# A hybrid attention layer on one core: lower parts of the memory weights on VectorE, sample queries stored once, own places for short pairs, first mix rows and output weights loaded two steps ahead

## The chip, the core and the metric

The kernel runs on one core of a Trainium2 chip. A core has TensorE (PE, matrix products; its weight loads are shown as PEld), VectorE (DVE), ScalarE (ACT) and GpSimd (POOL), and SyncE (SP), from whose queue this kernel issues all its DMA transfers. The metric is the device time in microseconds (us) of one execution; a time is the median of several runs.

## The reference, cut to what matters

One layer of a streaming encoder, for a prompt of 1024 frames and a sample (decode) group of 64 frames that share the weights. Everything is in 32-bit floats, model width 1024.

```
h  = rms_norm(x, g1);  one projection h @ w_in -> q, k, v of 8 heads A and 8 heads B, and forget logits
oa = band attention (chunk + 8 previous chunks, relative bias)       # prompt; sample: 512 cached keys + 64
ob = forgetting attention (bias = cumulated log sigmoid, causal)     # prompt; sample: 1024 cached keys + 64
x  = x + concat(oa, ob) @ w_o
mk, mv = split(rms_norm(mem_prompt, g_mem) @ w_mkv);  mk = rms_norm(mk)     # 256 memory rows; prompt only
x  = x + attend(rms_norm(rms_norm(x, g2) @ w_mq), mk, mv) @ w_mo
x  = x + (silu(causal_conv(gate)) * value) @ w_down,   gate, value = rms_norm(x, g3) @ w_up
```

Outputs: both groups' y, the new keys, values and forget logs, the memory keys and values, the convolution's state.

## The kernel before, in words

**Products in parts.** Most products are computed from two rounded parts of each operand, `hi` (rounded, by ACT) and `lo` (the remainder: raw minus `hi`, by DVE or POOL), in three products `hi*hi`, `hi*lo`, `lo*hi`.

**Stages.** (1) Projection and prompt attention, pair by pair: eight pairs `p` of two heads (0 to 3 are A, 4 to 7 are B). The sample's 64 frames are projected behind the prompt's; `proj_sample` (L353) normalises their queries and keys in a tile `qk` of four heads (two of q, two of k), in which every 64 numbers stand twice (`a` in `p h a d`), and its `store` (L376) writes them to a buffer `sqk` in HBM, and the values to `sv`. (2) From about 572 us on, the memory projection (L637), woven with the last prompt heads and then with the eight sample pairs. (3) The output product with `w_o` (L951), from 686 us on, then memory queries, memory attention, `w_mo`, the feed-forward layer.

**Memory projection.** `w_mkv` is cut into eight blocks `n` of 256 columns; for each block there are two row tiles `t`, and each (n, t) has four pieces of six matmuls. A list `line` holds the 64 pieces, and one entry more for the last key tile. The four quarters `y` of a block's weights are split ahead by `split_wm(n, y)` (L623): ACT writes `hi` (tile `mwhi`, L629), and `lo` (tile `mwlo`, L630) goes to DVE for odd `y` and to POOL for even `y`. Block 0 is split beside the last projection, block n+1 in the pieces of (n, t = 1).

**Sample pairs.** `Sample.load` (L756) brings queries and keys (`sqd`), new values (`svn`), cached keys (`kraw`) and cached values (`vraw`), all on SP. `prep` (L783) has POOL copy two heads at a time out of the doubled layout into `pair` (L789), PE transpose them (L790) into a bank `tq`, ACT and DVE scale the result (L795, L796); for pairs of kind B POOL also adds to the bias rows (L799, L802). `score` (L805) makes the logits and the exponential (L813 to L826), `turn` and `sum` transpose the probabilities and multiply by the values (L837 to L851, scaled at L857), `out` writes the mixed rows to `smix` (L861, L863). The pairs run in the order `SAMPLES = (4, 7, 5, 6, 0, 1, 3, 2)`: the first four from pool `mp`, the last four, which have the short cache of 512 keys, from pool `mq`. A loop over `x` from 0 to 8 takes one pair in each step; it loads pair x + 3 and gives each step `PER[x]` pieces of the memory line. With these numbers the memory line ends with step 6.

**The opening of the output product.** In step 7, `open_left` (L979) closes the left pools and opens on their place the weight stream (`Stream`, L915, raw tiles `raw`, three places, parts made at L932 and L933), the parts `a` of the mixed rows and the raw places `mraw` (`STAGE` = 10). The prompt's mixed rows lie in an HBM buffer `mixd`, eight tiles of 128 rows; they are taken in three chunks of columns (`CHUNKS`), so 24 loads `n`, chunk by chunk. Ten are loaded at once, and `split_mix(n)` (L998; ACT L1001, DVE L1002) loads n + 10 behind itself. The first product, chunk 0 of output tile 0, needs the eight split rows of that chunk and two weight tiles of `w_o`.

**What sets the order.** Each engine runs its queue in order. The program's order is a starting point: the queues are laid out when the program is built, and an instruction can stand before one that the code has earlier. `weave` and `place` spread secondary work over the pieces of a product. `tc.issue_after` keeps the loads in its block behind a given transfer.

## Time and profile before

| | |
|---|---|
| Median of 3 runs | 1759.43 us (1755.65 to 1760.1) |
| The profiled execution | 1761.79 us, of which the span is 1760.0 us |
| Mean granted clock of TensorE | 0.995 |
| Busy share PE, PEld | 97%, 94% |
| Busy share DVE, ACT, POOL | 67%, 52%, 36% |
| DMA | 196.70 MB, mean 112 GB/s |
| Memory projection (L637) | 572.0 to 679.4 us |
| Sample pairs' scores (L813) | 611.5 to 681.9 us |
| Output product (L951, first matmul) | 686.1 us |

How to read the rows. A timeline row gives start, duration, engine, line, operation, out<-in by the program's names, the number of merged instructions, and in brackets the idle time before it with what ended it. A waits row gives the total in us, the times, the longest. A stretch row gives start and end, length, busy time of PE, PEld, DVE, ACT and POOL with their instructions, the granted clock of TensorE, the mean busy share of the 16 DMA engines, and GB/s. A transfer row gives the count, KB each, and the median us from issue to landing. "SPq" is SP's queue.

### The profile page before, as it was taken

What the parts mean: (1) busy time and instruction counts of PE and PEld (TensorE: products, weight loads), DVE (VectorE), ACT (ScalarE), POOL (GpSimd) and SP (SyncE); (2) the same over time, 40 slices, a digit from 0 to 9 for tenths busy, and PEclk for the clock granted to TensorE, in tenths of its full rate; (3) what the DMA queues carried; (4) which work ended last, traced back from release to release, by engine and by line L of the source; (5) the groups of instructions that cost most, each with busy time, mean ns of one, the idle gap of its engine ahead of it and who ended that gap; (6) DMA issues with size and microseconds to landing.
All of it is one profiled execution on the core that took longest, in us unless ns stands there. A gap on an engine that the chain in (4) does not pass through costs nothing.

```text
span 1760.0 us, 33766 instructions
## 1 busy us (share of the span) xinstructions
PE 1700.5 (97%) x12376; PEld 1652.9 (94%) x12376; DVE 1180.9 (67%) x2591; ACT 920.2 (52%) x2030; POOL 629.4 (36%) x933
## 2 busy tenths in 40 slices
PE   7898999999999999999999999999999999999999
PEld 6788999999998888999999999999999999999999
DVE  5768667677677745333444389777777777659996
ACT  6756667677677656434555455433333334434442
POOL 3557667779778531553433512000000000000000
PEclk9999999999999999999999999999999999999999
DMA  7322222222233676531112662222222222793332
GB/s 253 93 64 59 66 73 72 62 75 62 61 105 95 200 218 207 183 116 43 49 54 69 176 214 72 92 80 86 82 74 74 75 74 74 255 337 120 113 105 88
DMA packets 135670, 196.70 MB, mean 112 GB/s; under 512 B 21240, under 2 KB 77688, under 8 KB 135504
## 3 DMA queue, kind: packets, MB, share of 16 engines
q1 hardware_dynamic: 135504, 194.55, 35.2%
q8 instruction: 97, 1.59, 0.4%
q14 instruction: 69, 0.57, 0.1%
HBM read 152.20 MB, written 45.44 MB: 112 GB/s over the span
## 4 chain that ended last, share of the span: by engine, by line
PE 46%; DVE 4%; issue 2%; ACT 1%; DMA 1%; POOL 1%; SPq 0%; DVEq 0%; ACTq 0%; POOLq 0%
PE W L1481 25%; PE W L1805 10%; PE pj L951 7%; PE S L1224 1%; PE tq L1260 1%; PE O L1260 1%; POOL lo L933 1%; DVE f L1346 1%; PE PT L1247 0%; DVE lo L1346 0%; ACT hi L1345 0%; DMA f<-x2d 0%; PE O L1224 0%; DMA x2d<-qhi 0%; DMA raw<-in_w_down_dram 0%
## 5 line engine op out<-in xcount | busy, mean ns | idle before, releaser
L310 PE MATMUL pj<-whi,xhi 128*128 128x384 f32 (+1 forms) x512 | 194.1, 379 | 2.3 <-DVE flog L325 1.6
L310 PE MATMUL pj<-wlo,xhi 128*128 128x384 f32 (+1 forms) x512 | 175.7, 343 | 4.5 <-POOL wlo L131 4.3
L310 PE MATMUL pj<-whi,xlo 128*128 128x384 f32 (+1 forms) x512 | 174.8, 342 | 0.7 <-DVE xlo L139 0.7
L1587 POOL COPY s<-gp 128x2 f32<-128x2 f32 x22 | 15.8, 720 | 335.9 <-DVE gp L1586 335.9
L1481 PE MATMUL W<-h,hi 128*128 128x272 f32 x704 | 134.4, 288 | 1.4 <-ACT qlo L1617 1.4
L515 ACT ACTIVATE s<-s,mx 128x640 f32<-128x640 f32 (+7 forms) x128 | 94.4, 738 | 75.4 <-DVE mx L513 74.7
L1805 PE MATMUL W<-f,hi 128*128 128x272 f32 x672 | 127.3, 287 | 0.0
L552 DVE TENSOR_TENSOR ptl<-PT,pth 128x512 fp32r<-128x512 f32 (+2 forms) x192 | 99.5, 522 | 35.5 <-ACT pth L551 33.6
L1481 PEld LDWEIGHTS W<-h,hi 128*128 128x128 f32 x704 | 110.8, 188 | 1.7 <-ACT qlo L1617 1.6
L1805 PEld LDWEIGHTS W<-f,hi 128*128 128x128 f32 x672 | 105.3, 188 | 0.2
L551 ACT CAST pth<-PT 128x512 fp32r<-128x512 f32 (+2 forms) x192 | 84.9, 449 | 38.9 <-PE PT L550 37.2
L310 PEld LDWEIGHTS pj<-wlo,xhi 128*128 128x128 f32 x512 | 98.5, 192 | 6.4 <-POOL wlo L131 6.0
L310 PEld LDWEIGHTS pj<-whi,xhi 128*128 128x128 f32 x512 | 98.3, 192 | 4.1 <-DVE flog L325 1.9
L1481 PE MATMUL W<-h,lo 128*128 128x272 f32 x352 | 101.8, 289 | 0.0
L310 PEld LDWEIGHTS pj<-whi,xlo 128*128 128x128 f32 x512 | 97.3, 190 | 1.8 <-DVE xlo L139 1.6
L1805 PE MATMUL W<-f,lo 128*128 128x272 f32 x336 | 96.8, 288 | 0.2 <-DVE lo L1346 0.2
L1345 ACT CAST hi<-raw 128x512 fp32r<-128x512 f32 x68 | 42.2, 621 | 102.2 <-PE W L1481 59.0
L550 PE MATMUL PT<-ident,s 128*128 128x128 f32 x528 | 89.6, 275 | 5.3 <-DVE ptl L552 5.3
L510 PE MATMUL S<-kh,q 128*128 128x256 f32 (+1 forms) x304 | 76.5, 277 | 16.6 <-DVE mx L513 16.5
L951 PE MATMUL pj<-a,hi 128*128 128x384 f32 (+1 forms) x352 | 86.9, 332 | 3.4 <-ACT hi L932 2.6
L518 POOL TENSOR_SCALAR s<-s,ssum 128x640 f32<-128x640 f32 (+6 forms) x96 | 70.8, 738 | 41.1 <-DVE ssum L516 30.0
L550 PEld LDWEIGHTS PT<-ident,s 128*128 128x128 f32 x528 | 65.4, 140 | 14.9 <-DVE ptl L552 9.1
(542 smaller groups left out, 5933.0 us busy)
## 6 DMA issues: line engine op xcount, KB each, us to landing
raw<-in_w_down_dram SPq DMA_DIRECT2D x45, 256.0 KB, 3.0
wraw<-in_w_dram SPq DMA_DIRECT2D x56, 192.0 KB, 2.5
raw<-in_w_up_dram SPq DMA_DIRECT2D x41, 256.0 KB, 2.8
h<-ad SPq DMA_DIRECT2D x32, 272.0 KB, 5.3
mwraw<-in_w_mkv_dram SPq DMA_DIRECT2D x16, 512.0 KB, 4.6
raw<-in_w_mo_dram SPq DMA_DIRECT2D x32, 256.0 KB, 3.3
kvraw<-in_w_down_dram SPq DMA_DIRECT2D x32, 256.0 KB, 3.5
ad<-t SPq DMA_DIRECT2D x22, 272.0 KB, 2.1
```

Source lines behind the costliest of these rows:

```text
L310: pe.matmul(pj[:, :nw], x_part(a, k, t * P, P), wt[k][b][:, :nw], start=n == 0, stop=n == 3 * KT - 1)
L510: pe.matmul(sp[:, a:a + (k1 - k0) * P], q, kk[:, h, src], start=m == 0, stop=m == 1)
L515: act.activation(s[:, :n], s[:, :n], ACT.Exp, bias=mx, scale=-1.0, accum_out=sm)
L518: pool.tensor_scalar(s[:, :n], s[:, :n], sm, 1.0, op0=ALU.mult, op1=ALU.mult)
L550: pe.transpose(pt[:, b - ch[0]], self.s[j][:, (b - w0) * P:(b - w0 + 1) * P], ident)
L551: act.copy(hi[:, f:f + n, j], pt[:, f:f + n])
L552: dve.tensor_tensor(lo[:, f:f + n, j], pt[:, f:f + n], f32(hi[:, f:f + n, j]), op=ALU.subtract)
L951: pe.matmul(out()[:, :cn], w[a][:, k % 4], x[b][k][:, c0:c0 + cn], start=k == 0 and (a, b) == SPLIT[0], stop=k == KT - 1 and (a, b) == SPL ...
L1260: pe.matmul(op[:, a0:a1], v[x][:, b, d * P:(d + 1) * P], self.p2[y][:, b, a0:a1], start=n == 0, stop=n == 5)
L1345: act.copy(hi, t)
L1481: pe.matmul(w[:, z, :Q], a(p, j), rights[j][b][:, z * Q:z * Q + Q], start=fresh and begin and j == 0 and x == 0, stop=final and end and j ...
L1805: pe.matmul(ws[m][:, z, :Q], la[p][:, m * P:(m + 1) * P], ra[b][:, z * Q:z * Q + Q], start=first and y == 0 and what in opening, stop=fina ...
```

## The change

Five edits, none of which changes what is computed.

1. `split_wm`: the lower parts of blocks 1 to 7 are all on DVE; block 0 stays as it was.
2. `sqk` has 256 columns instead of 512: each query and key head is stored once, and `sqd` has [64, 4, 64] numbers.
3. `prep` transposes straight from `sqd`; the tile `pair` and its 16 copies on POOL go.
4. The tiles of the sample pairs get more places: in `mp` three for `sqd` and `svn` instead of two; in `mq` four each for `sqd`, `svn`, `kraw` and `vraw`, as many as it has pairs.
5. `load_early`, called in steps 5 and 6, loads one output weight tile and four mixed rows of chunk 0 each, into places of their own in `mq`. `Stream` starts with the two weight tiles; `load_mix` leaves out n < 8, so that the opening of step 7 loads rows 8 to 17; the splits of rows 0 to 7 load nothing behind them.

```diff
-    sqk = dram.tile([8, S, 512], F32, name="sqk")
+    sqk = dram.tile([8, S, 256], F32, name="sqk")
...
-            nc.sync.dma_start(sqk[p], qk[:S].rearrange("p h a d -> p (h a d)"))
+            nc.sync.dma_start(sqk[p].rearrange("t (h d) -> t h d", h=4), qk[:S, :, 0])
...
-        (dve if y % 2 else pool).tensor_tensor(lo, raw, f32(hi), op=ALU.subtract)
+        (dve if n or y % 2 else pool).tensor_tensor(lo, raw, f32(hi), op=ALU.subtract)
...
-            self.qd = self.pl.tile([S, 4, P], F32, name="sqd", bufs=2)
+            self.qd = self.pl.tile([S, 4, 64], F32, name="sqd", bufs=3 if self.early else 4)
...
-            self.vraw = self.pl.tile([S, 2, 64], F32, name="svn", bufs=2)
+            self.vraw = self.pl.tile([S, 2, 64], F32, name="svn", bufs=3 if self.early else 4)
...
-            self.k = self.pl.tile([P, self.ctx], F32, name="kraw", bufs=3)
+            self.k = self.pl.tile([P, self.ctx], F32, name="kraw", bufs=3 if self.early else 4)
...
-                raw = self.pl.tile([P, 4, 2, 64], F32, name="vraw", bufs=6 if self.early else 3)
+                raw = self.pl.tile([P, 4, 2, 64], F32, name="vraw", bufs=6 if self.early else 4)
...
-            heads = self.qd.rearrange("t (x h) (a d) -> t x h a d", x=2, a=2)
             for x in range(2):
-                self.pair = self.pl.tile([S, 2, 64], F32, name="pair", bufs=2)
-                pool.tensor_copy(self.pair, heads[:, x, :, 0])
-                pe.transpose(tq[:, x, :S], self.pair.rearrange("t h d -> t (h d)"), ident[:S, :S])
+                pe.transpose(tq[:, x, :S], self.qd[:, 2 * x:2 * x + 2].rearrange("t h d -> t (h d)"), ident[:S, :S])
...
-            self.pl, self.raws, self.tiles, self.n = pl, [], {}, 0
+            self.pl, self.raws, self.tiles, self.n = pl, early_raws, {}, 0
...
-        raws = {}
+        raws = dict(enumerate(early_mix))
...
         def load_mix(n):
+            if n < KT:
+                return
...
-            if n + STAGE < 3 * KT:
+            if KT <= n and n + STAGE < 3 * KT:
                 load_mix(n + STAGE)
...
-            for n in range(4):
+            for n in range(KT, KT + STAGE // 2):
                 load_mix(n)
             stream.fetch()
-            for n in range(4, STAGE):
+            for n in range(KT + STAGE // 2, KT + STAGE):
                 load_mix(n)
...
+    early_mix, early_raws = [], []
+
+    def load_early(n):
+        if n < 2:
+            raw = mq.tile([P, 4, P], F32, name="oraw", bufs=3)
+            nc.sync.dma_start(raw, srcs[n])
+            early_raws.append(raw)
+        for k in range(4 * n, 4 * n + 4):
+            raw = mq.tile([P, 384], F32, name="omix", bufs=KT)
+            nc.sync.dma_start(raw, mixd[k][:, 0:384])
+            early_mix.append(raw)
...
             samples[x + 3].load()
+        if x in (5, 6):
+            load_early(x - 5)
```

## The prediction

> **What bounds the kernel now.** I read the page first, then the waits of TensorE between 560 and 710 us, where every edit lies, then stretches of that stage, then each engine's order of time around the largest gaps.

> ```profile
> span 1760.0 us, 33766 instructions
> PE 1700.5 (97%) x12376; PEld 1652.9 (94%) x12376; DVE 1180.9 (67%) x2591; ACT 920.2 (52%) x2030; POOL 629.4 (36%) x933
> ```

> TensorE (PE) is busy 97% of the span, and after 690 us it is practically never idle. So a change here is worth what it takes off PE's idle time, plus what PE loses at a lower granted clock, and nothing else. The gain then goes through to the end, because everything behind is work that PE does without gaps.

> ```profile
> PE pj L951 <- ACT hi L932: 2.6, 1, 2.6
> PE pj L637 <- POOL mwlo L630: 2.3, 2, 1.6
> PE S L510 <- DVE mx L513: 2.2, 3, 1.0
> PE PT L550 <- DVE ptl L552: 1.5, 3, 0.7
> ...
> PE pj L951 <- DVE a L1002: 0.8, 1, 0.8
> ```

> These are sums in us, times, and the longest. The first and the last stand at the start of the output product, the second is the memory weights' lower parts on POOL, the two between are the last attention heads waiting for DVE.

> ```profile
> 560.00:580.00 20.00, 17.80 (x132) 16.70 (x130) 15.44 (x37) 16.35 (x36) 18.69 (x35) 1.00 0.40 110
> 580.00:600.00 20.00, 17.97 (x146) 17.07 (x147) 16.09 (x38) 13.82 (x36) 9.15 (x12) 1.00 0.70 193
> 644.00:648.00 4.00, 4.00 (x23) 4.00 (x23) 1.93 (x4) 1.29 (x2) 0.95 (x1) 0.59 1.03 281
> 658.00:661.00 3.00, 3.00 (x16) 3.00 (x16) 3.00 (x1) 1.53 (x4) 3.00 (x3) 0.51 0.00 0
> 650.00:676.00 26.00, 24.62 (x168) 21.63 (x168) 12.33 (x25) 13.78 (x37) 6.15 (x8) 0.93 0.41 129
> 676.00:690.00 14.00, 10.49 (x68) 8.48 (x67) 6.22 (x18) 10.25 (x27) 2.52 (x2) 1.00 0.88 272
> 690.00:700.00 10.00, 10.00 (x61) 9.43 (x60) 8.21 (x24) 8.03 (x26) 2.95 (x2) 1.00 0.82 275
> ```

> Columns: stretch, length, busy PE, PEld, DVE, ACT, POOL, granted clock, DMA share, GB/s. PE stands 3.5 us between 676 and 690 (14.00 - 10.49), and runs at 0.59 and 0.51 of its clock for 4 and 3 us in two stretches where it is otherwise full.

> **Lower parts on DVE.** Seven of the eight weight blocks have two of their four lower parts on POOL; 14 instructions move.

> ```profile
> 638.61 2.18 ACT L629 CAST mwhi<-mwraw 128x512 fp32r<-128x512 f32 x4
> ...
> 641.43 0.71 PE L851 MATMUL O<-vraw,pth 128*128 128x128 f32 x4
> 643.76 0.52 PE L637 MATMUL pj<-mwlo,mhi 128*128 128x256 f32 x1 [1.62 <-POOL mwlo L630]
> ...
> 657.39 0.50 PE L637 MATMUL pj<-mwlo,mhi 128*128 128x256 f32 x1 [0.70 <-POOL mwlo L630]
> ```
> ```profile
> 641.50 0.98 POOL L789 COPY pair<-sqd 64x128 f32<-64x128 f32 x2 [2.74 <-PE tq L790]
> 642.46 2.49 POOL L630 TENSOR_TENSOR mwlo<-mwraw,mwhi 128x512 fp32r<-128x512 f32 x2
> ...
> 656.08 4.97 POOL L630 TENSOR_TENSOR mwlo<-mwraw,mwhi 128x512 fp32r<-128x512 f32 x4
> ```
> ```profile
> 590.21 1.25 DVE L630 TENSOR_TENSOR mwlo<-mwraw,mwhi 128x512 fp32r<-128x512 f32 x1
> ...
> 622.23 0.68 DVE L630 TENSOR_TENSOR mwlo<-mwraw,mwhi 128x512 fp32r<-128x512 f32 x1
> ...
> 641.62 3.88 DVE L630 TENSOR_TENSOR mwlo<-mwraw,mwhi 128x512 fp32r<-128x512 f32 x2
> ...
> 655.05 6.55 DVE L630 TENSOR_TENSOR mwlo<-mwraw,mwhi 128x512 fp32r<-128x512 f32 x2
> ```

> At 638.61 ACT has begun the upper parts, but POOL's queue stands behind the pair copies, which wait for PE's transposes until 641.50. Only then come POOL's lower parts, 1.25 us each, and PE waits 1.62 us. DVE meanwhile needs 3.88 and 6.55 us for two of the same instruction while POOL works beside it, against 0.68 us alone at 622.23. With all four on DVE from 641.62 the first is ready at 642.3 (641.62 + 0.68) and the others every 0.7 us; PE is free at 642.14 (641.43 + 0.71). So 0.2 us of the 1.62 stay: **-1.4 us**. At 657.39 DVE has the first part at 655.7 (655.05 + 0.68), before PE wants it: **-0.7 us**. The rest of DVE's queue gets shorter at both places: four parts take 2.7 us where two took 3.88, eight take 5.4 us against 6.55 for two.

> The slow clock follows directly upon these two gaps: 4 us at 0.59 cost 1.6 us of PE time, 3 us at 0.51 cost 1.5, together 3.1 us. If the waits go, the nearest row for the clock is 1.00, as in the stretches 560 to 600 and 676 to 700, which have gaps too: **-3.1 us**, with zero as the other end. [...]

> Cost: where DVE is nearly full, between 580 and 600 us (16.09 of 20), two parts come to it, 2 x 0.68 = 1.4 us, and 1.25 - 0.68 = 0.6 us go because POOL no longer works beside them, net 0.8 us. PE's waits for DVE there are the 2.2 and 1.5 us above, so not each us of DVE reaches PE. Between 0 and 0.8 I take half: **+0.4 us**. POOL, 18.69 of 20 busy before 580, is relieved at the same time, which could pay that back; I leave that gain in the range.

> **Queries stored once, pair copies gone.**

> ```profile
> sqk<-qk SPq DMA_DIRECT2D x8, 128.0 KB, 2.2
> ...
> sqd<-sqk SPq DMA_DIRECT2D x8, 128.0 KB, 3.9
> ```

> Eight stores and eight loads carry 64 KB each instead of 128, the stores in four pieces of 256 bytes a row. PE transposes straight from the loaded tile, in the same shape. The 16 copies on POOL go; what they did harm to was only the queue behind them, which the first edit empties as well. Bounds: a store that took twice its 2.2 us would still be many us ahead of the load of its pair, since the pairs are loaded two steps ahead; a saving of up to 1 us on POOL reaches nobody. **0.**

> **Own places.** A load of sample queries, values or keys no longer waits on SP's queue for a place in use. PE's list of waits names no such load, since the samples are loaded two steps ahead. **0**, apart from what follows.

> **Early mix rows and output weights.** In the eighth sample step the output product begins:

> ```profile
> 683.03 0.48 PE L851 MATMUL O<-svn,ptl 64*128 64x128 f32 x2
> 686.07 0.97 PE L951 MATMUL pj<-a,hi 128*128 128x384 f32 x4 [2.55 <-ACT hi L932]
> ...
> 689.13 0.63 PE L951 MATMUL pj<-a,hi 128*128 128x384 f32 x2 [0.81 <-DVE a L1002]
> ```
> ```profile
> 681.80 1.75 ACT L1001 CAST a<-mraw 128x384 fp32r<-128x384 f32 x4
> ...
> 685.40 0.62 ACT L932 CAST hi<-raw 128x512 fp32r<-128x512 f32 x1 [1.07 <-DMA raw<-in_w_o_dram]
> ...
> 690.43 0.59 ACT L841 COPY pth<-PT 128x512 f32<-128x512 f32 x1 [0.49 <-PE PT L837]
> ```
> ```profile
> 676.48 2.76 SPq L996 DMA_DIRECT2D mraw<-mixd  x6
> 679.35 0.45 SPq L763 DMA_DIRECT2D svn<-sv  x1
> 679.84 0.59 SPq L996 DMA_DIRECT2D mraw<-mixd  x1
> 680.59 1.28 SPq L924 DMA_DIRECT2D raw<-in_w_o_dram  x3
> ```

> The weights are issued at 680.59 and reach ACT at 685.40; PE stands 2.55 us for them and 0.81 us later on. With weights and rows long there, the two waits of 3.4 us are the upper end. What is late next is ACT: from 681.80 on it casts rows and weights and serves the last sample, and its own idle time there is 1.07 us for the weights and 0.49 us. PE cannot get more ahead than ACT does unless the casts change their order: ACT's idle time, 1.6 us, is the nearest row. The lower end is 1.1, the wait for the weights alone. **-1.5 us.** The stretch 690 to 700, where ACT is at 8.03 of 10 and PE at 10.00, says that PE then keeps the head start only as far as ACT does, so I go no higher.

> Ten transfers move to the fifth and sixth step (counted from zero): eight of 192 KB, two of 256 KB, 2.1 MB, ten issues on SP at 0.46 us (2.76 / 6). Between 650 and 676 the DMA share is 0.41, against 0.88 between 676 and 690. At the 272 GB/s of that later stretch they need 7.7 us of the 26, and 4.6 us of SP. They stand on SP beside the last two bias loads and the stores of the memory values; the code loads a bias one whole sample step ahead of its use, and that step covers the 2.3 us of five issues. **0**; without that cover 2.3 us.

> **Sum** against the profiled execution, 1761.79 us (span 1760.0 and 1.8 around it): -1.4 - 0.7 - 3.1 + 0.4 - 1.5 = -6.3, thus 1755.5 us. That execution lies 2.4 us over the median of the runs shown, 1759.43, so the median should go to **1753.1 us**, -0.36%. About 0.3%, 5.3 us, is what a measurement of this kernel can tell from no change.

> **The rivals.**
> 1. *As summed*, 1751.2 to 1754.7 us, between the neighbouring cases. Chance 0.44.
> 2. *The clock is hit by phase.* The timed runs lie between 1755.65 and 1760.1 us, 4.4 us apart, more than 3.1 us; so some of them may have lost nothing to the clock here. If the median run has half the loss, the gain is 6.3 - 1.6 = 4.7 us, with none 3.2 us: 1754.7 to 1756.2, within 0.3%. It speaks for it that the larger gap of 2.55 us kept 1.00; against, that the profiled one, with both slow stretches, is only 2.4 us over the median. [...] Chance 0.24.
> 3. *Hidden or given back.* DVE takes the whole 0.8 us, and ACT's order puts the sample's work ahead of the casts as now, so that the start of the product gains nothing: 1.4 + 0.7 - 0.8 = 1.3 us and at best half the clock: 1756.6 to 1758.1. For it: ACT is busy from 681.80 on; against: PE's row at 686.07 names the weight's cast. Chance 0.13.
> 4. *The early rows turn ACT's order round.* The weight is cast before 683.5 and both waits go whole: 1.9 us more than summed (3.4 - 1.5), 1751.2, and down to 1749 if POOL's relief also takes half of the 3.7 us that PE waits for DVE. Chance 0.10.
> 5. *Slower: DVE's queue stands for the casts.*

> ```profile
>   POOL mwlo L630: 5.1, 2
>   DVE mwlo L630: 0.3, 1
> ```

>    These rows say who waited for the upper parts' casts on ACT: POOL 5.1 us in two waits, DVE 0.3. If the moved parts are queued as early on DVE as they were on POOL, each such wait stops what is behind it there: the attention's mx and ptl, for which PE waits at once. Spread over 14 instructions the gain of 6.3 us is eaten at 0.45 us each, and slower by 0.3% from 0.83 us each (11.6 / 14); 5.1 us on two of them would still be a small gain. Against it stands DVE's 0.3 us for the 16 parts that it has now. With 12 us lost: 1765 us. Chance 0.09.

> **Range and chances.** The first case has its own range of 1751.2 to 1754.7. To hold 8 in 10 the range takes in the second and the third on one side and part of the fourth on the other: 1749.5 to 1759.0. Faster by over 0.3% (below 1754.1): most of the first and all of the fourth, 0.48. Within 0.3%: the rest of the first, the second and the third, 0.43. Slower by over 0.3%: the fifth, 0.09.

> **What the changed profile would show.** Right: no wait of L637 for mwlo above 0.3 us, the clock at 1.00 between 640 and 680, DVE's L630 at 0.68 us in all 30 instances, no POOL row at L789; the first L951 starting within 1.5 us of the last L851 before it, ACT not waiting for the weights, and DMA share up between 650 and 676. Wrong: new waits of PE for DVE before 615 us, L932 still behind the exponential of the last sample with PE standing over 2 us, or a slow clock at another gap. The forecast also fails if the queues of the whole stage come out in another order, which no row of before can tell.

## The result, and the profile after

The changed kernel takes 1752.11 us (median of 7 runs, 1751.11 to 1754.42), the kernel before 1758.9 us in the same session (7 runs, 1755.65 to 1761.55): ratio 0.9962, 95% interval 0.9952 to 0.9972. The forecast was 1753.1 us, in a range of 1749.5 to 1759.0. The profiled execution took 1754.42 us. In the changed kernel's rows the lines behind the edits have other numbers: the transposes of the queries are L787 (before L790), the scores L810 (L813), the products with the values L848 (L851), the transposes of the probabilities L834 (L837), the mixed rows' copies L860 (L863), the output weights' parts L929 and L930 (L932, L933), the output product L948 (L951), the mixed rows' parts L1000 and L1001 (L1001, L1002). L630 and L637 keep theirs.

The page of the changed kernel:

```profile
span 1752.5 us, 33723 instructions
PE 1698.6 (97%) x12376; PEld 1650.5 (94%) x12376; DVE 1182.6 (67%) x2605; ACT 920.8 (53%) x2030; POOL 608.0 (35%) x903
```

POOL has lost 21 us of work (629.4 to 608.0) and DVE has gained 1.7 us only, for 14 instructions of 0.68 us (9.5 us): DVE was being held up beside POOL before (up to 3.25 and 5.85 us for one such instruction, where POOL worked beside it). TensorE's waits between 540 and 710 us, sums in us, times, longest:

```profile
PE PT L550 <- DVE ptl L552: 1.9, 2, 1.5
PE S L510 <- DVE mx L513: 1.9, 3, 1.0
PE pj L948 <- DVE a L1001: 1.3, 2, 0.7
PE S L810 <- ACT sq L792: 0.8, 2, 0.6
PE PT L742 <- DVE kv L723: 0.5, 1, 0.5
...
PE pj L948 <- ACT hi L929: 0.2, 1, 0.2
```

The wait of L637 for POOL's lower parts (2.3 us) is gone, and the wait of 2.6 us for the first output weight is down to 0.2; a wait of 1.3 us for DVE's part of the mixed rows stands where 0.8 stood. The stretches of the changed kernel (length; busy PE, PEld, DVE, ACT, POOL; granted clock, DMA share, GB/s):

```profile
650.00:676.00 26.00, 25.19 (x181) 21.66 (x180) 10.41 (x33) 16.31 (x44) 0.00 (x0) 1.00 0.65 207
676.00:690.00 14.00, 12.50 (x74) 10.34 (x72) 12.89 (x27) 13.51 (x38) 6.14 (x4) 1.00 0.65 203
```

The clock is 1.00 in both, as in every stretch between 560 and 720. ACT is at 13.51 of 14 while the output product opens, where it was at 10.25.

Where the time went is read best from landmarks. The group of the products with `mwlo`, before and then after; the last two numbers ahead of the shape are its first and last start:

```profile
L637 PE MATMUL pj<-mwlo,mhi x128: 278/282/517, 573.3 to 679.3; 128*128 128x256 f32 x128
```
```profile
L637 PE MATMUL pj<-mwlo,mhi x128: 274/282/386, 574.5 to 673.6; 128*128 128x256 f32 x128
```

The memory projection takes 106.0 us before and 99.1 after: 6.9 us gone. From its end to the second output tile (first L951 or L948 into `PT`, 698.1 and 691.1) it is 18.8 before and 17.5 after, 1.3 us more. The first landmark came 1.2 us later. Of that, 0.7 us is one wait of TensorE for DVE ahead of it (`ptl`, 1.48 us where it was 0.75); the rest is of the first stage, which the change hardly touches, and in the 13 profiles of this case the landmark lies anywhere between 569.7 and 575.5. What is left, 0.5 us, is behind the second output tile. So I compare these two lengths below, not ends.

The projection's 6.9 us can be taken apart. As stretches, before and then after:

```profile
573.30:679.30 106.00, 98.59 (x714) 88.22 (x713) 60.27 (x149) 58.19 (x154) 37.52 (x61) 0.97 0.66 192
```
```profile
574.50:673.60 99.10, 95.70 (x713) 85.33 (x712) 57.58 (x161) 58.28 (x153) 17.30 (x32) 1.00 0.75 219
```

TensorE stands 7.4 us (106.00 - 98.59) before and 3.4 us after, 4.0 us less: 2.3 us are the two waits for POOL's lower parts, 1.7 us are smaller ones. The clock was at 0.50 for twice 3.41 us before and never after, which makes 3.4 us. The two add up to 7.4; against that, TensorE's other busy time is 0.5 us longer.

### The profile page after: what moved, and what is told of

The parts are those of the page before. It is cut to its first block, busy times and chain, and to the rows that moved or that the text cites. A ratio compares the mean times of both kernels' runs of the same rounds, so it can differ in the third digit from the quotient of the medians.

```text
span 1752.5 us, 33723 instructions
## 1 busy us (share of the span) xinstructions
PE 1698.6 (97%) x12376; PEld 1650.5 (94%) x12376; DVE 1182.6 (67%) x2605; ACT 920.8 (53%) x2030; POOL 608.0 (35%) x903
## 4 chain that ended last, share of the span: by engine, by line
PE 50%; DVE 2%; issue 1%; POOL 1%; ACT 0%; DMA 0%; DVEq 0%; POOLq 0%; ACTq 0%
PE W L1494 26%; PE W L1818 13%; PE pj L948 7%; PE S L1237 1%; PE tq L1273 1%; PE O L1273 1%; POOL lo L930 1%; PE W L948 1%; PE PT L1260 0%; DVE lo L930 0%; PE O L1237 0%; PE PT L1218 0%; DVE qhi L1346 0%; POOL s L1252 0%; ACT hi L929 0%
## 5 line engine op out<-in xcount | busy, mean ns | idle before, releaser
L552 DVE TENSOR_TENSOR ptl<-PT,pth 128x512 fp32r<-128x512 f32 (+2 forms) x192 | 99.5, 521 | 34.9 <-ACT pth L551 33.0
L550 PE MATMUL PT<-ident,s 128*128 128x128 f32 x528 | 89.6, 276 | 5.7 <-DVE ptl L552 5.5
L510 PE MATMUL S<-kh,q 128*128 128x256 f32 (+1 forms) x304 | 76.2, 277 | 16.3 <-DVE mx L513 16.2
L948 PE MATMUL pj<-a,hi 128*128 128x384 f32 (+1 forms) x352 | 87.9, 333 | 1.8 <-DVE a L1001 1.3
L550 PEld LDWEIGHTS PT<-ident,s 128*128 128x128 f32 x528 | 65.5, 141 | 15.2 <-DVE ptl L552 9.4
```

The lines of the kernel that those rows point to most:

```text
L510: pe.matmul(sp[:, a:a + (k1 - k0) * P], q, kk[:, h, src], start=m == 0, stop=m == 1)
L550: pe.transpose(pt[:, b - ch[0]], self.s[j][:, (b - w0) * P:(b - w0 + 1) * P], ident)
L552: dve.tensor_tensor(lo[:, f:f + n, j], pt[:, f:f + n], f32(hi[:, f:f + n, j]), op=ALU.subtract)
L948: pe.matmul(out()[:, :cn], w[a][:, k % 4], x[b][k][:, c0:c0 + cn], start=k == 0 and (a, b) == SPLIT[0], stop=k == KT - 1 and (a, b) == SPL ...
```

## The experiments

Each is the kernel before with the edit named, if nothing else is said, timed against the kernel before in its own session. "Projection" is the length of the memory projection, "opening" the time from its end to the second output tile, both in the profiled run; "slow clock" counts the stretches of some 3.4 us in which the clock was at 0.50 between 640 and 664 us.

| run | median (range, runs) | ratio (95% interval) | projection | opening | slow clock |
|---|---|---|---|---|---|
| before | | | 106.0 | 18.8 | 2 |
| changed kernel | 1752.11 (1751.11-1754.42, 7) | 0.9962 (0.9952-0.9972) | 99.1 | 17.5 | 0 |
| d1 lower parts only | 1753.6 (1751.89-1754.84, 5) | 0.9962 (0.995-0.9973) | 99.3 | 17.9 | 0 |
| d2 all but lower parts | 1753.73 (1752.55-1755.68, 5) | 0.9963 (0.9951-0.9975) | 101.0 | 17.5 | 0 |
| d3 all but early loads | 1753.62 (1750.05-1756.1, 6) | 0.9961 (0.9949-0.9973) | 99.1 | 17.9 | 0 |
| d4 early loads only | 1759.09 (1756.1-1762.27, 11) | 0.9999 (0.9989-1.0008) | 106.0 | 17.5 | 2 |
| e1 changed kernel again | 1752.75 (1751.38-1754.49, 6) | 0.9968 (0.9956-0.9979) | 99.1 | 17.5 | 0 |
| e2 no pair copies | 1754.04 (1751.28-1756.65, 11) | 0.9976 (0.9967-0.9985) | 100.0 | 17.8 | 0 |
| e3 own places only | 1759.58 (1756.15-1761.07, 11) | 1.0004 (0.9995-1.0013) | 105.6 | 17.5 | 1 |
| e4 filled waits | 1752.74 (1751.94-1753.95, 6) | 0.9967 (0.9956-0.9979) | 101.2 | 17.6 | 0 |
| f1 four places for pair | 1754.64 (1752.16-1757.26, 7) | 0.9969 (0.9958-0.998) | 100.1 | 17.6 | 0 |
| f2 before again | 1760.8 (1 run) | | 104.6 | 18.9 | 1 |
| x1 opening's lower parts on DVE | 1751.74 (1749.3-1754.97, 5) | 0.9951 (0.9937-0.9964) | 99.1 | 17.2 | 0 |

The kernel before had medians of 1759.81 us beside d1 to d4, 1758.61 beside e1 to e4 and 1759.34 beside f1, x1 and f2.

### One part at a time (d1 to d4)

d1 is the first edit by itself:

```diff
-        (dve if y % 2 else pool).tensor_tensor(lo, raw, f32(hi), op=ALU.subtract)
+        (dve if n or y % 2 else pool).tensor_tensor(lo, raw, f32(hi), op=ALU.subtract)
```

> The kernel before with the first edit alone (lower parts of blocks 1 to 7 on DVE; pair copies, places and loads as before). Theory (the terms of the prediction): 1.4 + 0.7 us of waits and up to 3.1 us of slow clock go, DVE gives 0.4 back, so -4.8 us against before, and no wait of L637 for mwlo. Rival, clock by phase: only -1.7 to -3.2 us, since the runs of before lose less than 3.1 us to the clock. Rival, the opening also profits: the changed profile has its memory products ending 5.7 us earlier and the opening giving only about 1 us, so nearly all of the -6.8 us is this edit: -5.5 us or more.

d2 is the changed kernel with that line put back:

```diff
-        (dve if n or y % 2 else pool).tensor_tensor(lo, raw, f32(hi), op=ALU.subtract)
+        (dve if y % 2 else pool).tensor_tensor(lo, raw, f32(hi), op=ALU.subtract)
```

> The changed kernel with the lower parts of even quarters back on POOL. Theory, as the prediction has it: what is left is the opening, -1.5 us against before, and L637 waits for POOL again with the clock falling after it. Rival, the pair copies were the cause: POOL's queue no longer stands behind copies that wait for PE, so its lower parts come 2 to 3 us sooner, the 1.62 us wait goes without the first edit, and the time is within 2 us of the changed kernel (-5 us).

d3 is the changed kernel without the fifth edit, d4 the kernel before with the fifth edit alone:

```diff
+        if x in (5, 6):
+            load_early(x - 5)
```

> The changed kernel without the early loads: the ten loads stand in the opening as before. Theory: the first four edits give -4.8 us against before, and the opening again stands 2.5 us for the weights' cast and 0.8 us for DVE, so +1.5 us against the changed kernel. Rival, the opening is hidden or was helped by the free SP queue alone: within 0.5 us of the changed kernel. Rival, the head start is kept whole: +2.7 us, which is what the first output matmul gained beyond the end of the memory products in the changed profile.

> The kernel before with the early loads alone. Theory: the waits at the opening go as far as ACT lets them, -1.5 us against before; the waits of L637 for POOL and the slow clock stay. Rival, the early loads need the own places: SP's queue still stands for places of the short pairs, the early rows land late and the opening gains less than 0.5 us. Rival, ten more issues on SP before the last bias loads cost a wait: 0 or slower.

The parts do not add up. d1 takes off 6.2 us, d2, which leaves out just that part, 6.1 us as well, and d3 6.2. So the moved parts are sufficient but not needed: something in edits 2 to 4 removes the same loss. d4 gains nothing that can be measured: its opening is 1.3 us shorter in the profile, which its interval (0.9989 to 1.0008, so at most 1.9 us less) can't tell from zero. The profile of d4 shows what it kept. POOL's queue, and then TensorE's:

```profile
639.56 0.98 POOL L789 COPY pair<-sqd 64x128 f32<-64x128 f32 x2 [3.76 <-PE tq L790]
640.52 2.49 POOL L630 TENSOR_TENSOR mwlo<-mwraw,mwhi 128x512 fp32r<-128x512 f32 x2
```
```profile
641.82 0.38 PE L637 MATMUL pj<-mwlo,mhi 128*128 128x256 f32 x1 [1.63 <-POOL mwlo L630]
```

POOL stands 3.76 us at the copies into `pair`, which wait for TensorE's transposes of the pair before; the lower parts that TensorE needs next stand behind them in the same queue. Two remedies come to mind, and the change has both: take the lower parts off that queue (edit 1), or take the copies off it (edit 3). The next runs ask whether this is it.

### The pair copies, the places, and the clock (e1 to e4)

e1 is the changed kernel once more. e2 is edits 2 and 3: queries stored once, `pair` and its copies gone, all lower parts and places as before. e3 is edit 4, the places alone. e4 keeps everything of the kernel before and adds 12 and 6 matmuls with a tile of zeros, which add nothing to the sums, at the first piece of blocks 5 and 6, to fill TensorE's two waits:

```diff
+            if m == 0 and t == 0:
+                for _ in range({5: 12, 6: 6}.get(n, 0)):
+                    pe.matmul(mpj[n, t][:, :256], zr, wm[n, 0][0][:, 0], start=False, stop=False)
```

> The changed kernel once more, beside the variants of this study. Theory after the first four runs: lower parts on DVE and the end of the pair copies each release the same 5 us, the early loads add 0.4 us by the trace (the end of the memory products to the second output tile: 17.4 us in the changed kernel, 17.8 without early loads); so about -6.5 us against before, the same as the three variants within 1 us. Rival, the parts add up: at least 1.5 us faster than the variant without early loads (which was at 0.9961 of before).

> The kernel before with queries stored once and no pair copies; lower parts, places and early loads as before. Theory, the copies stood ahead of the lower parts in POOL's queue and waited there for PE: the 1.62 us and 0.70 us waits and the slow clock go, -5 us against before. Rival, it is the places: the copies do no harm by themselves and the waits stay, 0 us. Rival, POOL's own length: lower parts of 1.28 us on POOL keep PE waiting whatever stands ahead, -1 us at most.

> The kernel before with more places for the sample pairs' loads alone. Theory, no load of them is on PE's path: 0 us, with L637 still waiting for POOL and the clock falling behind it. Rival, the samples' loads come sooner and shift the whole stage: -2 us or more, with POOL's lower parts earlier.

> The kernel before with 12 and 6 more matmuls of 128x256 in the pieces where L637 waits for POOL (blocks 5 and 6), which multiply by a tile of zeros and add nothing to the sums; they are work of 1.4 and 0.7 us that PE does instead of standing. Theory, the slow clock is paid for standing: the waits on POOL are mostly filled, the clock stays at 1.00 between 640 and 665, and 3 us of slow clock go, -2 to -3 us against before although PE has 18 matmuls more. Rival, the slow clock has another cause (the DVE and POOL work beside it, the time since the start): it stays at 0.5 for 3 to 4 us after the same places, and the time is that of before or up to 2 us longer.

e2, without the copies, loses both waits for `mwlo` and 4.6 us; e3 loses neither. POOL's queue in e2:

```profile
635.63 2.51 POOL L630 TENSOR_TENSOR mwlo<-mwraw,mwhi 128x512 fp32r<-128x512 f32 x2 [0.62 <-DMA svn<-sv]
643.45 1.28 POOL L630 TENSOR_TENSOR mwlo<-mwraw,mwhi 128x512 fp32r<-128x512 f32 x1 [5.30 <-ACT mwhi L629]
```

POOL now waits for ACT's upper parts, which it needs, and no longer for TensorE, and it is in time. So it was not POOL's speed: the same two instructions, of the same 1.25 us each, on the same engine, are early enough once nothing stands ahead of them.

e4 did not test the clock by itself, as it was meant to. The added matmuls changed the layout of the queues, and POOL's lower parts came to stand ahead of the copies (in its listing L794 is the copy):

```profile
637.46 2.54 POOL L630 TENSOR_TENSOR mwlo<-mwraw,mwhi 128x512 fp32r<-128x512 f32 x2 [1.10 <-issue]
647.93 0.52 POOL L794 COPY pair<-sqd 64x128 f32<-64x128 f32 x2 [7.93 <-PE tq L795]
```

So the waits vanished rather than being filled. By accident this is a third way to the same gain (5.9 us) with copies, lower parts and places as before and 18 matmuls more: what stands ahead of the lower parts in POOL's queue is what counts.

### The copies stay but need not wait (f1)

e2 and e4 took the copies out of the way. f1 leaves copies, lower parts and their order, and takes away only what the copies wait for:

```diff
-                self.pair = self.pl.tile([S, 2, 64], F32, name="pair", bufs=2)
+                self.pair = self.pl.tile([S, 2, 64], F32, name="pair", bufs=4)
```

> The kernel before with one edit: pair has four places instead of two; the copies, POOL's lower parts and everything else stay, and in POOL's queue the copies still stand ahead of the two pairs of lower parts. Theory (a copy that waits for its place holds up POOL's queue): no wait of L637 for mwlo over 0.5 us, POOL's idle time before the copies for the transposes gone (3.3 us in one row before), first to last L637 mwlo 100 to 102 us instead of 106, and the time 4 to 6 us below before (0.9966 to 0.9977). Rival A (POOL's load is the matter: its lower parts are slow beside DVE and it has too much to do): the waits for mwlo stay at 1 us or more, time within 0.1% of before. Rival B (the copies' positions alone matter, whether they wait or not): half the gain, 2 to 3 us.

TensorE's, DVE's, ACT's and SP's queues are those of the kernel before, and POOL's differs in the places of a few copies; as many copies as before, twelve and fourteen, stand ahead of the two groups of lower parts that TensorE waited for, and the first group still follows two of them. POOL in f1 (in the kernel before, the row of these copies is the one at 641.50 us in the prediction, with 2.74 us of waiting):

```profile
635.13 0.28 POOL L789 COPY pair<-sqd 64x128 f32<-64x128 f32 x1
...
635.95 0.28 POOL L789 COPY pair<-sqd 64x128 f32<-64x128 f32 x1
637.15 2.51 POOL L630 TENSOR_TENSOR mwlo<-mwraw,mwhi 128x512 fp32r<-128x512 f32 x2 [0.91 <-POOL pair L789]
```

The products with `mwlo` as a group of TensorE between 540 and 710 us, in the kernel before and in f1 (total, mean ns; idle time ahead of them and what ended it):

```profile
L637 PE MATMUL pj<-mwlo,mhi 128*128 128x256 f32 x128 | 38.3, 299 | 2.3 <-POOL mwlo L630 2.3
```
```profile
L637 PE MATMUL pj<-mwlo,mhi 128*128 128x256 f32 x128 | 36.7, 287 | 0.0
```

No wait is left, the mean matmul is 12 ns shorter since none runs at half clock, the projection is 5.9 us shorter and the kernel 4.7 us faster. One digit gives 4.7 us, where all five edits give 6.8 and, in e1, 5.9. Rival A of f1 (POOL's load) falls, and rival B (place in the queue, whether the copies wait or not) too: its 2 to 3 us lie outside the interval (0.9958 to 0.998, at least 3.5 us). Not every wait of a copy is gone: the next two, at 645.52, still follow 5.86 us of waiting for TensorE. But the lower parts behind them then wait 2.50 us more for ACT, so that wait holds up nothing.

### The clock: the kernel before again (f2)

> The kernel before once more, for a second profile: the waits for mwlo recur at 1.5 to 1.7 and 0.7 us or thereabouts. Theory (whether such a wait costs clock is a matter of phase): one or none of the two slow stretches, at other places than in the first profile. Rival (the wait's length decides): slow at 0.5 for about 3.4 us after each of the two, as in the first.

The waits recur almost to the hundredth. TensorE in f2, and then its stretches:

```profile
644.86 0.39 PE L637 MATMUL pj<-mwlo,mhi 128*128 128x256 f32 x1 [1.63 <-POOL mwlo L630]
...
656.98 0.39 PE L637 MATMUL pj<-mwlo,mhi 128*128 128x256 f32 x1 [0.71 <-POOL mwlo L630]
```
```profile
643.00:646.00 3.00, 1.37 (x12) 1.18 (x11) 3.00 (x2) 0.26 (x1) 3.00 (x3) 1.00 1.05 360
646.00:649.00 3.00, 3.00 (x28) 3.00 (x27) 1.03 (x4) 1.92 (x4) 0.05 (x1) 1.00 0.97 288
658.00:661.00 3.00, 3.00 (x16) 3.00 (x15) 3.00 (x1) 1.14 (x2) 2.64 (x3) 0.50 0.00 1
```

The same wait of 1.62 to 1.63 us was followed by half clock (0.50) in the first profile of before and in d4, and by full clock (1.00) here and in e3. So the wait's length does not decide it, and the rival falls. The second wait was followed by half clock in all four (0.70 or 0.71 us long in three of them, 1.68 us in e3). The clock's record shows a grid: in the first profile of before and in that of the changed kernel every stretch at half clock is 3.41 or 6.83 us long (but for the last, which the end of the record cuts), and begins a whole multiple of 3.413 us behind the one ahead of it (in the first profile of before at 643.87 and 657.52 us, four times 3.413 apart). The stretches between 640 and 664 us are 3.40 to 3.42 us long in d4, e3 and f2 as well, and begin at 642.28 and 655.92, at 656.86 and at 657.94 us, so the grid lies elsewhere in each of these executions. Laid on that grid, the steps around the first wait are these, in the first profile of before and then in f2:

```profile
640.46:643.87 3.41, 1.51 (x11) 1.05 (x9) 3.41 (x7) 1.43 (x4) 2.37 (x4) 1.00 1.01 334
643.87:647.28 3.41, 3.41 (x16) 3.41 (x17) 2.06 (x4) 1.29 (x2) 1.08 (x1) 0.50 1.04 298
```
```profile
640.87:644.28 3.41, 2.08 (x16) 1.63 (x15) 3.41 (x7) 2.11 (x5) 1.69 (x3) 1.00 0.99 322
644.28:647.70 3.42, 2.84 (x24) 2.84 (x25) 2.59 (x3) 0.94 (x1) 1.77 (x2) 1.00 0.96 327
```

In before, and in d4 too, the whole wait lies in one step, in which TensorE stands 1.9 us in before (3.41 - 1.51), and the next step runs at 0.50. In f2 the end of a step cuts the wait, 1.33 us of standing fall into one step and 0.58 into the next, and the clock stays at 1.00; in e3 it is cut as well (at 643.2 us, four times 3.413 ahead of 656.86). So the wait's place on the grid goes with the clock in these four executions; no run shows why. How much standing is enough stays open: in the first profile of before 1.38 us in the step from 654.10 to 657.52 us, that of the second wait, was followed by 0.50, while 1.86 us in the step from 43.11 to 46.53 us was followed by 1.00. In that profile the waits ahead of half clock between 640 and 664 us were 1.62 us in one piece, and 0.68 and 0.70 us close together.

Within this stage f2 has one more such stretch, behind the first output matmul's wait of 2.41 us for the weight, where the prediction's gap of 2.55 us had left the clock at 1.00:

```profile
685.20:688.60 3.40, 3.06 (x10) 2.91 (x11) 1.49 (x2) 3.30 (x10) 2.52 (x2) 0.51 1.02 357
```

That goes with the grid too: in the first profile of before the end of a step at 684.8 us (643.87 + 12 x 3.413) cuts the gap, while in f2 2.1 of the 2.41 us lie ahead of the end of a step at 685.2 us. And f2's opening of 18.9 us has some 1.5 us of half clock in it (3.06 x 0.49, an estimate): the length of an opening in one execution is known no better than that.

### The lower parts of the opening on DVE (x1)

The changed kernel, with the output weights' first four lower parts on DVE too:

```diff
-                (dve if self.n >= 48 else pool).tensor_tensor(lo, raw, f32(hi), op=ALU.subtract)
+                (dve if self.n < 4 or self.n >= 48 else pool).tensor_tensor(lo, raw, f32(hi), op=ALU.subtract)
```

> The changed kernel with the lower parts of the output weights' first four tiles on DVE instead of POOL as well. Theory (in the opening POOL's subtractions and DVE's hold each other up, 2.58 us for a row of 0.6): DVE's L1001 rows near 0.6 to 0.7 us there, PE's two waits for a (0.58 and 0.68) gone, the second output tile 0.5 to 1 us earlier, time 0 to 1 us below the changed kernel, 1751.1 to 1752.7. Rival (ACT sets the opening, at 13.5 of 14 us): no change in the second output tile, time the same to 0.3 us, or up to 0.7 us later since DVE has four more parts before a.

In the changed kernel DVE and POOL are slow beside each other there (DVE's three parts take 2.58 us, in x1 0.51 to 0.56 us each; POOL's subtraction takes 1.44 us, the next one 1.28), and TensorE waits for DVE:

```profile
677.47 2.58 DVE L1001 TENSOR_TENSOR a<-omix,a 128x384 fp32r<-128x384 f32 x3
```
```profile
677.73 1.44 POOL L930 TENSOR_TENSOR lo<-oraw,hi 128x512 fp32r<-128x512 f32 x1 [40.39 <-DMA mraw<-mixd]
```
```profile
677.65 0.44 PE L948 MATMUL pj<-a,hi 128*128 128x384 f32 x1 [0.23 <-ACT hi L929]
...
679.64 0.61 PE L948 MATMUL pj<-a,hi 128*128 128x384 f32 x2 [0.58 <-DVE a L1001]
...
682.19 0.62 PE L948 MATMUL pj<-a,hi 128*128 128x384 f32 x2 [0.68 <-DVE a L1001]
```

In x1 DVE's rows are short, and both waits for `a` are gone:

```profile
678.44 1.02 DVE L1001 TENSOR_TENSOR a<-omix,a 128x384 fp32r<-128x384 f32 x2
679.39 0.68 DVE L930 TENSOR_TENSOR lo<-oraw,hi 128x512 fp32r<-128x512 f32 x1
...
680.07 0.54 DVE L1001 TENSOR_TENSOR a<-omix,a 128x384 fp32r<-128x384 f32 x1
```

But the second output tile comes only 0.3 us earlier (17.2 against 17.5), not the 0.5 to 1 expected: most of the 1.3 us of waiting comes back elsewhere. A wait of 0.42 us for ACT's copy of the mixed rows (L860) is new, and ACT is busy 13.76 of the 14 us from 676 on, so that ACT sets the pace there is likely, but no run shows it. x1 has the lowest median, 1751.74 us, but its interval overlaps with those of the changed kernel; that it is better is not shown.

## Why the prediction was right, step by step

The total was right: 6.3 us forecast, 6.8 measured beside the changed kernel and 5.9 in e1. The mechanism (waits for lower parts behind the pair copies on POOL, and the clock behind these waits) was right as well. That the sum came so close is in part luck: the early loads gave 0.4 us at most instead of 1.5, and 1.7 us of smaller waits in the projection, which no term has, made up for it. The steps:

- *Lower parts on DVE, -1.4 and -0.7.* Both waits went whole, 2.3 us, not 2.1: no L637 row waits any more. DVE's L630 was not at 0.68 us in all 30 instances:

```profile
L630 DVE TENSOR_TENSOR mwlo<-mwraw,mwhi x30: 669/683/1352, 548.3 to 657.3; 128x512 fp32r<-128x512 f32 x30
```

  The longest took 1.35 us; the median is as said.
- *The clock, -3.1.* Right for the profile compared (0.59 and 0.51 became 1.00; in whole, two stretches of 3.41 us at half clock, 3.4 us). For other executions the record has a mean granted clock for each timed run: one minus that, times the span, is the time lost if TensorE has work throughout. Averaged, it is 10.3 us over the 23 runs of before beside e1 and 7.0 over the six of e1, so 3.3 us less; over all 51 runs of before that have it and the 13 of the changed kernel it is 10.2 and 6.6. These are estimates, for the whole span, but they speak for the first case and against the second rival, which gave the median run half of the loss: the four profiles have 2, 2, 1 and 1 slow stretches between 640 and 664 us, and f2 one more in the opening. No run takes away the clock's share alone: e4 was to do it and did not.
- *DVE's cost, +0.4.* Seen in one row: `ptl`, whose sum goes from 1.5 to 1.9 us, with one wait of 1.48 us at 571.93 where it was 0.75. All five profiles with the first edit have it, and no other has. It is the new wait for DVE ahead of 615 us that the prediction named as a sign of being wrong, but its size is as forecast, and a wait of 0.56 us for `mx` at 577 goes. In the kernel before TensorE also had these:

```profile
PE PT L742 <- DVE kv L723: 1.2, 1, 1.2
...
PE PT L837 <- ACT smix L863: 0.7, 1, 0.7
```

  They fell by 0.7 and 0.4 us, and 0.4 us for `smx` went whole; a new wait for the scaled queries (L810) takes 0.8, of it 0.6 in the projection. With those for `mx` and `ptl` inside the projection, these make most of the 1.7 us of smaller waits above. The prediction had none of them.
- *Pair copies, 0.* Right only as "nothing more beside the first edit". The prediction named their harm, the queue behind them, and then gave the whole gain to edit 1. Alone, edits 2 and 3 are worth 4.6 us (e2). A reader who took the zero for the edit's value, and dropped the other edit, would have been wrong.
- *Own places, 0.* Right (e3).
- *Early loads, -1.5.* This term was mis-sized. The opening did get 1.3 us shorter, but d3, without the loads, has 0.9 of that, and e3, also without them, all of it; in company the loads add 0.4 us at most, less than the runs can tell (1752.11 against 1753.62 us, ratios of 0.9962 and 0.9961). A wait of 1.6 us for the weight is left in d3 where before had 2.6, and taking it away helps little, which fits ACT, at 13.51 of 14, as the next limit, as the prediction had it. The DMA share between 650 and 676 us rose from 0.41 to 0.65 as forecast, yet it is 0.55 in d3 and 0.63 in f1, which have no early loads, 0.46 in d4, which has, and 0.49 in f2: most of the rise goes with the shorter projection and is no sign of the early loads.

The first output matmul came right behind the last sample's (677.65 us, with L848 from 676.36 for 1.06 us and 0.23 us of waiting), ACT does not wait for the weights there, and there is no POOL row at L789's place. The fifth rival, DVE's queue standing for the casts, did not come: in the changed kernel DVE's L630 waited for ACT's upper parts twice, 0.5 us in all.

## What to carry to other kernels

An instruction on an in-order queue that waits for the engine it is meant to help holds up everything behind it (POOL's copies into `pair` waited 2.74 us in before and 3.76 us in d4, with the lower parts behind them); look at what stands ahead of the late instruction, in the bracket of the row before it, ahead of asking whether its engine is too slow. Here two more buffers for a helper tile gave 4.7 us, where a five-part change gave 5.9 to 6.8. When several edits can remove one and the same wait, price them alone and in company: their gains are not a sum, and leaving one out of the whole shows next to nothing for an edit that alone is worth nearly everything.

## What the runs showed of the hardware

DVE's subtractions of the lower parts took longer beside POOL's. Of two DVE subtractions in the first profile of before the first ended ahead of POOL's and took 0.68 to 0.71 us; the second took 3.25 us beside two of POOL's that followed one another and 5.85 us beside four (the rows at 641.62 and 655.05 us in the prediction have both together), and ended 0.55 to 0.56 us behind POOL's last each time. POOL's own stayed at 1.25 to 1.27 us there. DVE is not always kept out so: in f1 the longest of its sixteen subtractions took 1.77 us, and POOL's longest took 1.82 us. An earlier start did not help DVE: by the recorded starts the subtraction of 5.85 us began 0.33 us ahead of POOL's four (655.75 and 656.08 us) and still ended behind them.
